# Partition sums of ten modulation vectors: the summed array as stationary operand and two columns as moving one

## Chip, cores and metric

The kernel runs on one core of a Trainium2 chip. The metric is the device time of one execution in microseconds (us). Times of before are the median of 3 runs. One further execution was recorded by the hardware profiler; durations and waits below come from that one.

## What is computed

Two layers of a trunk over 512 latent and 256 context tokens of width 1024, all in float32. The part that matters here is the modulation at the head of each layer:

```python
sc = jax.nn.silu(c)
scc = jax.nn.silu(c_ctx)
for l in range(DEPTH):
    mod_x = (sc @ ada_w[l] + ada_b[l])[:, None, :]
    mod_y = scc @ ada_w[l] + ada_b[l]
    shx1, scx1, gx1, shx2, scx2, gx2 = jnp.split(mod_x, 6, axis=-1)
    shy1, scy1, gy1, shy2, scy2, gy2 = jnp.split(mod_y, 6, axis=-1)
    hx = rms_norm(x, norm1_g[l]) * (1.0 + scx1) + shx1
    hy = rms_norm(y, norm1_g[l]) * (1.0 + scy1) + shy1
...
    x = x + gx1 * (mx @ w_out[l])
```

So each layer multiplies a vector of 1024 (one for latent tokens, one for context tokens) with a 1024x6144 matrix. The result is six vectors of 1024 per kind of token: two shifts (sh1, sh2), two scales (sc1, sc2) and two gates (g1, g2). Shifts and scales are applied where a normalised block stands with features on partitions; gates multiply blocks with tokens on partitions. The rest of a layer is a combined input projection, four kinds of attention or retention ("the mixers" below), an output projection and a SwiGLU feed-forward part with 2816 hidden columns.

## The kernel before

**Projections.** Every large product is float32 made of three float32r products (`mm3`, L465 to L469): high part by high part, high by low, low by high. The low parts are made by `split_unit` (L446) with an ACT copy and a subtraction on DVE or POOL (L213). These products fill TensorE's (PE's) instruction stream from end to end.

**Modulation.** sh1 and sc1 of layer 0 are needed at once and have a path of their own (`ada_first`), which the change leaves alone. The other ten vectors go through `ada_sums` (L371). It works in pieces of 128x512 of the weights: a load on ACT's queue, then on DVE one multiply-add per kind of token (L395 the first, L397 the other seven) into an accumulator of 128x512. After eight pieces one half vector is left as 128 partial sums per column, which have to be added over the partitions. PE does that at L404: for each of four groups of 128 columns, and for each kind of token, the moving operand is the accumulator's 128 columns and the stationary operand is 32 columns of `ones` (a tile of zeros with one column of 1.0, so that token kind s lands in row s). The four groups go to four column tiles of the array (`tile_position=(0, 32*g)`), so that the sums of group g land on PSUM partitions 32g and 32g+1.

Context tokens leave after layer 0, so in layer 1 only sh1 and sc1 have two kinds of token; g1, sh2, sc2 and g2 have one. With two kinds a half vector takes eight products, with one it takes four; each float32 product is two instructions of PE. Below a run of 16 or of 8 such instructions is called a burst: twelve bursts of 16 (g1, sh2, sc2, g2 of layer 0; sh1, sc1 of layer 1; two halves each) and eight of 8.

**After the sums**, `ada_out` (L411) brings a vector into the form in which it is used:
- gates: a tile of zeros (L416, POOL), four loads of the bias (L419, SP's queue), an addition on 128x256 (L421, DVE), four stores to the DRAM tensor `mod_d` (L424, SP's queue). `gate_load` later reads them back, spread over all partitions.
- shifts and scales: a copy out of PSUM (L426, ACT), two transposes of 128x128 (L429, PE), two copies (L431, DVE) and, in `mod_finish`, an addition of the bias for each kind of token (L304, DVE), for scales also a multiply by the norm's gain (L306, DVE).

**Order.** The generators of `ada_sums` are fillers: those of g1 and sh2 run beside the second block of the input projection (columns 1440 to 1951), those of sc2 and g2 beside the block of columns 416 to 927 in the middle of the attention work, and those of layer 1 in the feed-forward part of layer 0 (`steps`, L1442), where the stream of PE is products only. A scheduler then puts the instructions of each engine in a fixed order; an engine works through its own strictly in that order. Tiles get addresses from a planner, and a change of the program moves both.

Of the kernel before, what the change touches and what calls it, by code (L numbers as in the profile page):

```python
# [16 lines left out]
P = 128  # L17
# [70 lines left out]
def build(tc, I, out, opts=None):  # L88
# [81 lines left out]
    AS = (opts or {}).get("as", 1)  # L170
    AD = [(lambda *a, x=x, **k: ada_sums(*a, atag=x, **k)) if x else (lambda *a, **k: ada_rest(*a)) for x in (opts or {}).get("ad", ('ldr', 'ldr'))]
    Q = {k: {"sp": sp, "act": act, "pool": pool}[(opts or {}).get("q", {}).get(k, DQ.get(k, "sp"))]
# [51 lines left out]
    identb = C("identb", [P, P], BF16)  # L224
    ones = C("ones", [P, 33])
    sink = C("sink", [P, LAYERS, H])
# [17 lines left out]
    def vec(name, k0=0, n=1):  # L244
        i, r = VROW[name]
        return vecs[i][:, r + k0:r + k0 + n]
# [52 lines left out]

    def mod_finish(l, v, s, k0, n):  # L300

        m = modT[l][:, s, SLOT[v], k0:k0 + n]
        b = vec("b%d" % l, VT.index(v) * 8 + k0, n)
        dve.tensor_tensor(m, m, b, op=ALU.add)  # L304
        if v[1] == "c":
            dve.scalar_tensor_tensor(m, m, 1.0, vec("g%s_%d" % (v[2], l), k0, n), op0=ALU.add, op1=ALU.mult)  # L306

    def ada_load(q, xs={}):
# [34 lines left out]

    def ada_rest(l, vs, wtag, depth, tag="u"):

        todo = [(v, hf, k) for v in vs for hf in range(2) for k in range(8)]
        W = {}

        def load(i):
            if i < len(todo):  # L350
                v, hf, k = todo[i]
                c0 = VT.index(v) * D + 512 * hf
                W[i] = T(wtag, [P, 512])
                Q["ada"].dma_start(W[i], I["ada_w"][l, k * P:(k + 1) * P, c0:c0 + 512])

        for i in range(depth):
            load(i)
        yield
        for i, (v, hf, k) in enumerate(todo):
            if k == 0 and hf == 0:  # L360
                ps = PS(tag)[:, 0:256]
            w = W.pop(i)
            for g in range(4):
                pe.matmul(ps[32 * g:32 * g + 32, hf * P:hf * P + P], sT[:, k, :], w[:, 128 * g:128 * g + 128],
                          start=(k == 0), stop=(k == 7), tile_position=(0, 32 * g))
            load(i + depth)
            if k == 7 and hf == 1:
                ada_out(l, v, ps, tag)
            yield

    def ada_sums(l, vs, wtag, depth, tag="u", atag="PT", after=None):  # L371
# [16 lines left out]
        for i, (v, hf, k) in enumerate(todo):  # L388
# [10 lines left out]
            if k == 7:  # L399
                if hf == 0:  # L400
                    ps = PS(tag)[:, 0:256]
                for g in range(4):
                    for s in range(ns):
                        pe.matmul(ps[32 * g:32 * g + 32, hf * P:hf * P + P], ones[:, 1 - s:33 - s],  # L404
                                  acc[s][:, 128 * g:128 * g + 128], start=(s == 0), stop=(s == ns - 1),
                                  tile_position=(0, 32 * g))
                if hf == 1:
                    ada_out(l, v, ps, tag)
            yield

    def ada_out(l, v, ps, tag):  # L411
        c0 = VT.index(v) * D
        rt = T(TR[0], [P, 256])
        if v[0] == "g":
            bt = T(TR[1], [P, 2, P])
            pool.memset(bt, 0.0)  # L416
            src = I["ada_b"][l, c0:c0 + D]
            for g in range(4):
                sp.dma_start(bt[32 * g:32 * g + 2],  # L419
                             bass.AP(tensor=src.tensor, offset=src.offset + P * g, ap=[[0, 2], [512, 2], [1, P]]))  # L420
            dve.tensor_tensor(rt, ps, bt.rearrange("p a b -> p (a b)"), op=ALU.add)  # L421
            for g in range(4):
# [388 lines left out]
    for l in range(LAYERS):  # L811
# [620 lines left out]
        v3 = I["ffn_w3"][l].rearrange("(k p) n -> p k n", p=P)  # L1432
        ada_todo = (ada_rest, ada_sums)[AS](1, VT, "qT", 3) if l == 0 else iter(())
        hn = {}
# [103 lines left out]
```

## Time and profile before

| | |
|---|---|
| median of 3 runs | 1904.59 us (1903.46 to 1905.05) |
| profiled execution, its own time | 1910.68 us |
| its span, first to last instruction | 1908.8 us, mean granted PE clock 0.985 |
| PE busy | 1811.7 us, 95% of the span |
| PE weight loads (PEld) | 1494.0 us, 78% |
| DVE busy | 1187.5 us, 62% |
| ACT busy | 672.9 us, 35% |
| POOL busy | 605.2 us, 32% |

PE executes weight loads and products as two streams that overlap. The recorded length of a product holds its way through the array, so that products that follow each other overlap in the record. What one costs in a full stream is therefore read from start to start, not from its length.

### The profile page before, as it was taken

Reading aid. Unit: us, or ns where it says so; the run is one execution under the profiler, and the core shown is the slowest. Engines: PE = TensorE matmul, PEld = TensorE weight load, DVE = VectorE, ACT = ScalarE, POOL = GpSimd, SP = SyncE. Lnnn points to the kernel's source line nnn. Section 1 sums busy time; section 2 is a strip of 40 time slices with the busy share of each in tenths; the row PEclk is TensorE's granted clock in tenths of the full one; section 3 lists DMA queues with packets and bytes.
Section 4 is the critical chain, followed back from the end, with each engine's and each line's share of the span. In section 5 each row is a group of like instructions: output and inputs, shape, how many; then the busy total and the mean of one; then the engine's idle time right before and its main releaser. Section 6 shows DMA issues by size and latency. Waiting matters only on the chain. (4 is left out here: it accounts for less than half of the span.)

```text
span 1908.8 us, 28192 instructions
## 1 busy us (share of the span) xinstructions
PE 1811.7 (95%) x10447; PEld 1494.0 (78%) x10447; DVE 1187.5 (62%) x2676; ACT 672.9 (35%) x1517; POOL 605.2 (32%) x560
## 2 busy tenths in 40 slices
PE   6899999889999999999999999899889999999997
PEld 3677777778889887888888878788777888888885
DVE  5696886877898757564434293465588863434335
ACT  3325643254542221221122233564255532222223
POOL 0211113323115443444344111211333144645542
PEclk9999999899999999999999999999999999999999
DMA  7675436445124346342222222422443033232321
GB/s 226 210 206 162 131 98 187 127 151 117 50 95 127 122 155 199 105 134 63 74 67 67 57 84 91 120 75 81 143 142 100 15 115 101 84 107 89 102 86 44
DMA packets 193555, 215.22 MB, mean 113 GB/s; under 512 B 66660, under 2 KB 141578, under 8 KB 193418
## 3 DMA queue, kind: packets, MB, share of 16 engines
q10 hardware_dynamic: 75840, 111.17, 18.8%
q1 hardware_dynamic: 117578, 102.25, 18.1%
q8 instruction: 82, 1.34, 0.3%
q14 instruction: 55, 0.45, 0.1%
HBM read 192.76 MB, written 20.63 MB: 112 GB/s over the span
## 5 line engine op out<-in xcount | busy, mean ns | idle before, releaser
L469 PE MATMUL pg<-wh,b 128*128 128x512 f32 (+2 forms) x1128 | 439.9, 394 | 7.2 <-POOL b L213 6.2
L467 PE MATMUL pg<-wh,b 128*128 128x512 f32 (+2 forms) x1128 | 443.1, 393 | 1.8 <-ACT b L515 0.9
L468 PE MATMUL pg<-wl,b 128*128 128x512 f32 (+2 forms) x1128 | 441.5, 391 | 2.2 <-DVE rs_yn L288 1.8
L467 PE MATMUL ps<-b,wh 128*128 128x512 f32 (+1 forms) x1120 | 388.2, 347 | 0.0
L469 PE MATMUL ps<-b,wl 128*128 128x512 f32 (+1 forms) x1120 | 386.7, 345 | 0.8 <-DVE wl L213 0.8
L468 PE MATMUL ps<-b,wh 128*128 128x512 f32 (+1 forms) x1120 | 386.9, 345 | 0.5 <-POOL b L213 0.5
L213 DVE TENSOR_TENSOR wl<-raw,wh 128x1024 fp32r<-128x1024 f32 (+1 forms) x131 | 207.4, 1592 | 174.9 <-ACT wh L449 145.3
L449 ACT ACTIVATE wh<-raw 128x1024 fp32r<-128x1024 f32 (+1 forms) x196 | 203.8, 1049 | 271.1 <-PE pg L469 172.3
L213 POOL TENSOR_TENSOR wl<-raw,wh 128x1024 fp32r<-128x1024 f32 (+1 forms) x65 | 160.0, 2462 | 336.7 <-ACT wh L449 286.8
L1362 POOL TENSOR_TENSOR b<-b,nat 128x512 f32<-128x512 f32 (+1 forms) x204 | 217.8, 1087 | 124.0 <-DVE nat L1360 95.0
L469 PEld LDWEIGHTS pg<-wh,b 128*128 128x128 f32 x1128 | 214.9, 191 | 49.6 <-POOL b L213 9.6
L467 PEld LDWEIGHTS pg<-wh,b 128*128 128x128 f32 x1128 | 215.5, 191 | 40.9 <-ACT b L1476 1.9
L468 PEld LDWEIGHTS pg<-wl,b 128*128 128x128 f32 x1128 | 215.2, 191 | 39.7 <-DVE rs_yn L288 2.3
L467 PEld LDWEIGHTS ps<-b,wh 128*128 128x128 f32 x1120 | 213.5, 191 | 27.4 <-issue 2.4
L469 PEld LDWEIGHTS ps<-b,wl 128*128 128x128 f32 x1120 | 213.4, 191 | 26.0 <-DVE wl L213 1.0
L468 PEld LDWEIGHTS ps<-b,wh 128*128 128x128 f32 x1120 | 213.6, 191 | 25.5 <-POOL b L213 0.7
L1360 DVE TENSOR_TENSOR nat<-pg,gate 128x512 f32<-128x512 f32 x240 | 161.9, 688 | 102.0 <-PE pg L469 97.8
L1473 ACT ACTIVATE P<-ps 128x512 f32<-128x512 f32 (+1 forms) x70 | 35.4, 505 | 224.3 <-PE ps L469 128.0
L1475 DVE TENSOR_TENSOR P<-ps,P 128x512 f32<-128x512 f32 (+1 forms) x70 | 40.1, 575 | 118.9 <-PE ps L469 118.8
L1476 ACT ACTIVATE b<-P 128x512 fp32r<-128x512 f32 (+1 forms) x70 | 37.6, 538 | 195.3 <-DVE P L1475 176.0
L397 DVE SCALAR_TENSOR_TENSOR PT<-qT,consts,PT 128x512 f32<-128x512 f32 x112 | 94.0, 857 | 14.6 <-DMA qT<-in_ada_w_dram 13.3
L213 POOL TENSOR_TENSOR b<-P,b 128x512 fp32r<-128x512 f32 (+1 forms) x24 | 27.8, 1158 | 231.9 <-ACT b L1476 231.9
(322 smaller groups left out, 2441.7 us busy)
## 6 DMA issues: line engine op xcount, KB each, us to landing
raw<-in_ffn_w_dram ACTq DMA_DIRECT2D x132, 512.0 KB
qT<-in_ada_w_dram ACTq DMA_DIRECT2D x96, 256.0 KB
raw<-in_w_in_dram SPq DMA_DIRECT2D x40, 512.0 KB
a<-in_ada_w_dram SPq DMA_DIRECT2D x32, 256.0 KB
a<-in_ada_w_dram ACTq DMA_DIRECT2D x32, 256.0 KB
xn<-in_ada_w_dram ACTq DMA_DIRECT2D x32, 256.0 KB
raw<-in_w_out_dram SPq DMA_DIRECT2D x16, 512.0 KB
ldq<-q_d SPq DMA_DIRECT2D x40, 128.0 KB
```

What stands on the lines that cost most here:

```text
L213: eng.tensor_tensor(out, full, hi.bitcast(F32), op=ALU.subtract)
L397: dve.scalar_tensor_tensor(acc[s], w, sS[:, k, s:s + 1], acc[s], op0=ALU.mult, op1=ALU.add)
L449: act.activation(hi, raw_ap, AF.Copy)
L467: pe.matmul(ps, a[0], b[0], start=first, stop=False)
L468: pe.matmul(ps, a[0], b[1], start=False, stop=False)
L469: pe.matmul(ps, a[1], b[0], start=False, stop=last)
L1360: dve.tensor_tensor(tm, ps, gates[(0 if t < 4 else 2) + b], op=ALU.mult)
L1362: eng.tensor_tensor(ap, ap, tm[:, a:c], op=ALU.add)
L1473: act.activation(s1[j][:, sl], ps, AF.Silu)
L1475: dve.tensor_tensor(s1[j][:, sl], ps, s1[j][:, sl], op=ALU.mult)
L1476: act.activation(gh[j][:, sl], s1[j][:, sl], AF.Copy)
```

## The change

In `ada_sums` the two operands change places. The accumulator's 128x128 group becomes the stationary operand, and two columns of `ones` (now 4 wide) become the moving one; no `tile_position` is given. The sums of a group then land on 128 PSUM partitions, in two columns (one per kind of token), which is the form in which shifts and scales are used. The number of products stays the same.

`ada_out` follows. A bias is read from `vecs`, where all biases already stand as columns. Shifts and scales need one addition straight from PSUM, and scales one multiply; copy, transposes and `mod_finish` are gone. Gates add the bias into a tile of 128x16, transpose it once (PE), copy the 16x128 result (ACT), and store it in two transfers; the tile of zeros and the four loads are gone. `ada_rest`, which no option in use selects, is deleted.

```diff
@@ ada_sums
                 if hf == 0:
-                    ps = PS(tag)[:, 0:256]
+                    ps = PS(tag)[:, 0:16].rearrange("p (k s) -> p k s", s=2)
                 for g in range(4):
                     for s in range(ns):
-                        pe.matmul(ps[32 * g:32 * g + 32, hf * P:hf * P + P], ones[:, 1 - s:33 - s],
-                                  acc[s][:, 128 * g:128 * g + 128], start=(s == 0), stop=(s == ns - 1),
-                                  tile_position=(0, 32 * g))
+                        pe.matmul(ps[:, 4 * hf + g, :], acc[s][:, 128 * g:128 * g + 128], ones[:, 1 - s:3 - s],
+                                  start=(s == 0), stop=(s == ns - 1))
@@ ada_out
-        rt = T(TR[0], [P, 256])
+        b = vec("b%d" % l, VT.index(v) * 8, 8).unsqueeze(1).to_broadcast([P, 2, 8])
+        sums = ps.rearrange("p k s -> p s k")
         if v[0] == "g":
-            bt = T(TR[1], [P, 2, P])
-            pool.memset(bt, 0.0)
-            src = I["ada_b"][l, c0:c0 + D]
-            for g in range(4):
-                sp.dma_start(bt[32 * g:32 * g + 2],
-                             bass.AP(tensor=src.tensor, offset=src.offset + P * g, ap=[[0, 2], [512, 2], [1, P]]))
-            dve.tensor_tensor(rt, ps, bt.rearrange("p a b -> p (a b)"), op=ALU.add)
-            for g in range(4):
-                dst = mod_d[l][:, c0:c0 + D].rearrange("s (h g f) -> s h g f", h=2, g=4)[:, :, g, :]
-                sp.dma_start(dst, rt[32 * g:32 * g + 2, :].rearrange("p (a b) -> p a b", a=2))
+            m = S("adag", 16, bufs=2)
+            dve.tensor_tensor(m.rearrange("p (s k) -> p s k", s=2), sums, b, op=ALU.add)
+            pt = PS(tag)[0:16, 0:P]
+            pe.transpose(pt, m, ident)
+            rt = T(TR[0], [P, P])[0:16, :]
+            act.activation(rt, pt, AF.Copy)
+            for s in range(2):
+                sp.dma_start(mod_d[l][s, c0:c0 + D].rearrange("(k f) -> k f", f=P), rt[8 * s:8 * s + 8, :])
         else:
-            act.activation(rt, ps, AF.Copy)
-            pt = PS(tag)[:, 0:256].rearrange("p (a b) -> p a b", a=2)
-            for b in range(2):
-                pe.transpose(pt[:, b, :], rt[:, b * P:(b + 1) * P], ident)
-            for s in range(2):
-                dve.tensor_copy(modT[l][:, s, SLOT[v]].rearrange("p (h g) -> p h g", h=2), pt[:, :, s::32])
-                mod_finish(l, v, s, 0, 8)
+            m = modT[l][:, :, SLOT[v]]
+            dve.tensor_tensor(m, sums, b, op=ALU.add)
+            if v[1] == "c":
+                dve.scalar_tensor_tensor(m, m, 1.0, vec("g%s_%d" % (v[2], l), 0, 8).unsqueeze(1).to_broadcast([P, 2, 8]),
+                                         op0=ALU.add, op1=ALU.mult)
```

The scheduler's order moves with it. In the first place below, PE's order in the feed-forward part of layer 0 behind the second half of sc1 of layer 1 (`PT` are accumulators, `consts` holds `ones` and the identity, `ps` are the products of the feed-forward part), before:

```order
L404 MATMUL pu_7576<-PT_7585,consts 32x128
L404 MATMUL pu_7576<-PT_7586,consts 32x128
L467 MATMUL ps_7977<-b_1446_6238,wh_7873 128x512
L468 MATMUL ps_7977<-b_1448_6240,wh_7873 128x512
L469 MATMUL ps_7977<-b_1446_6238,wl_7874 128x512
L429 MATMUL pu_7961<-consts,nat_7959 128x128 x2
L467 MATMUL ps_7977<-b_1446_6238,wh_7873 128x512
```

and after, where lines from `ada_out` on have smaller numbers (L467 to L469 have become L429 to L431, and the sums stand at L369):

```order
L369 MATMUL pu_7543<-consts,PT_7552 128x2
L369 MATMUL pu_7543<-consts,PT_7553 128x2
L429 MATMUL ps_7935<-b_1444_6213,wh_7840 128x512
L430 MATMUL ps_7935<-b_1446_6215,wh_7840 128x512
L431 MATMUL ps_7935<-b_1444_6213,wl_7841 128x512
L429 MATMUL ps_7935<-b_1444_6213,wh_7840 128x512
```

The sums stand at the same place in PE's order, and the two transposes behind them are gone.

The second place is PE's order behind the second half of g1 of layer 1, in the same part, before:

```order
L469 MATMUL ps_8429<-b_1447_6239,wl_8327 128x512
L404 MATMUL pu_8103<-PT_8164,consts 32x128 x4
L467 MATMUL ps_8481<-b_1418_6094,wh_8332 128x256
L468 MATMUL ps_8481<-b_1419_6095,wh_8332 128x256
L469 MATMUL ps_8481<-b_1418_6094,wl_8333 128x256
```

and after:

```order
L431 MATMUL ps_8387<-b_1445_6214,wl_8285 128x512
L369 MATMUL pu_8061<-consts,PT_8122 128x2 x4
L429 MATMUL ps_8435<-b_1416_6069,wh_8290 128x256
L430 MATMUL ps_8435<-b_1417_6070,wh_8290 128x256
L431 MATMUL ps_8435<-b_1416_6069,wl_8291 128x256
L384 MATMUL pu_8425<-consts,adag_8423 16x128
```

Here a transpose has come in, three products behind the sums; it reads a tile that DVE writes in between.

The third place is DVE's order at the end of the first gate, g1 of layer 0 (`ldq` are accumulators, `a` pieces of weights, `pu` the sums), before:

```order
L395 TENSOR_SCALAR ldq_1174<-a_237_1131,consts 128x512
L421 TENSOR_TENSOR nat_1053<-pu_971,nat_1054 128x256
L395 TENSOR_SCALAR ldq_1175<-a_237_1131,consts 128x512
```

and after:

```order
L362 SCALAR_TENSOR_TENSOR ldq_991<-a_210_1015,consts,ldq_991 128x512
L1155 TENSOR_SCALAR kd_2994<-kd_2994 128x8
L382 TENSOR_TENSOR adag_1053<-pu_971,consts 128x16
L360 TENSOR_SCALAR ldq_1095<-a_211_1022,consts 128x512
```

The addition has moved up by one half vector: it now stands almost directly behind the multiply-add that completes the accumulator (`ldq_991`) from which PE makes its sums, where before it stood behind all of the next vector's first half. In the mixers of layer 0 the order of all engines shifts in many small places; from the feed-forward part of layer 0 on, PE's order differs only where sums and transposes stand.

## Rows read from the trace of the kernel before

**Rows 1.** Busy us by stretch: PE, PEld, DVE, ACT, POOL; PEclk, DMA share, GB/s.

```profile
96.00:143.00 47.00, 45.51 (x245) 33.48 (x244) 43.37 (x72) 13.51 (x37) 6.18 (x2) 1.00 0.73 206
220.00:312.00 92.00, 88.64 (x636) 67.79 (x635) 76.70 (x201) 45.92 (x144) 10.04 (x8) 1.00 0.39 119
312.00:430.00 118.00, 104.61 (x601) 88.42 (x600) 85.83 (x307) 47.90 (x127) 40.12 (x49) 0.91 0.50 154
617.00:993.00 376.00, 368.88 (x2018) 312.73 (x2017) 214.59 (x276) 74.30 (x105) 167.10 (x156) 1.00 0.37 116
```

**Rows 2.** Groups of the sums' line L404, layer 1 (columns: count, ns min/median/max, first and last start).

```profile
L404 PE MATMUL pu<-PT,consts x128: 272/273/298, 615.8 to 992.4; 128*32 128x128 f32 x128
```

**Rows 3.** Timeline of PE, a burst of 16 (start us, us, operation, partitions and columns).

```profile
615.48 0.28 PE L468 MATMUL ps<-b,wh 128*128 128x256 f32 x1
615.60 0.28 PE L469 MATMUL ps<-b,wl 128*128 128x256 f32 x1
615.80 0.66 PE L404 MATMUL pu<-PT,consts 128*32 128x128 f32 x16
...
616.73 0.39 PE L468 MATMUL ps<-b,wh 128*128 128x512 f32 x1
616.96 0.39 PE L469 MATMUL ps<-b,wl 128*128 128x512 f32 x1
```

**Rows 4.** The same view, a burst of 8.

```profile
740.71 0.28 PE L469 MATMUL ps<-b,wl 128*128 128x256 f32 x1
...
741.62 0.40 PE L468 MATMUL ps<-b,wh 128*128 128x512 f32 x1
```

**Rows 5.** The same view, a burst of layer 0, which stands in two pieces.

```profile
97.78 0.39 PE L467 MATMUL pg<-wh,b 128*128 128x512 f32 x1
98.10 0.41 PE L404 MATMUL pu<-ldq,consts 128*32 128x128 f32 x2
...
99.10 0.66 PE L404 MATMUL pu<-ldq,consts 128*32 128x128 f32 x14
...
100.02 0.60 PE L693 MATMUL pu<-consts,nat 128*128 128x128 f32 x4
```

**Rows 6.** Timeline of PE's weight loads in the retention part: float32, 128 columns.

```profile
366.52 0.53 PEld L1282 LDWEIGHTS ps<-ldr,P 128*128 128x128 f32 x4
366.97 0.30 PEld L1278 LDWEIGHTS ps<-b,rt 128*128 128x128 f32 x2
367.19 0.19 PEld L1282 LDWEIGHTS ps<-ldr,P 128*128 128x128 f32 x1
```

**Rows 7.** Timeline of PE, the way out of such a run into products.

```profile
355.75 0.43 PE L467 MATMUL pg<-wh,b 128*128 128x416 f32 x1
356.02 0.35 PE L468 MATMUL pg<-wl,b 128*128 128x416 f32 x1
356.20 0.35 PE L469 MATMUL pg<-wh,b 128*128 128x416 f32 x1
```

**Rows 8.** Timeline of PE, a pair of the transposes that go.

```profile
141.07 0.40 PE L468 MATMUL pg<-wl,b 128*128 128x512 f32 x1
...
141.76 0.39 PE L467 MATMUL pg<-wh,b 128*128 128x512 f32 x1
```

**Rows 9.** Waits in 617 to 993 us (total, times, longest us).

```profile
PE pu L429 <- ACT nat L426: 3.5, 2, 2.7
```

**Rows 10.** Timeline of ACT ahead of the longer of these waits.

```profile
723.35 0.38 ACT L1473 ACTIVATE P<-ps 128x256 f32<-128x256 f32 x1 [7.32 <-DVE PT L395]
```

**Rows 11.** Busy time by stretch, columns as in the first group: a stretch at half clock.

```profile
569.85:573.25 3.40, 3.40 (x18) 3.40 (x18) 2.14 (x6) 0.42 (x1) 0.73 (x1) 0.50 0.06 24
337.75:354.80 17.05, 12.43 (x54) 11.10 (x54) 11.99 (x37) 1.47 (x3) 1.40 (x3) 0.50 0.26 77
```

**Rows 12.** Groups of lines L421 and L424 (columns as in the second group).

```profile
L421 DVE TENSOR_TENSOR nat<-pu,nat x4: 420/424/425, 121.8 to 992.8; 128x256 f32<-128x256 f32 x4
L424 SPq DMA_DIRECT2D mod_d<-nat x16: 232/255/283, 122.3 to 994.2; - x16
```

More of the change, by code (lines that the diff above doesn't have):

```diff
@@ L170, in build @@
     AS = (opts or {}).get("as", 1)
-    AD = [(lambda *a, x=x, **k: ada_sums(*a, atag=x, **k)) if x else (lambda *a, **k: ada_rest(*a)) for x in (opts or {}).get("ad", ('ldr', 'ldr'))]
+    AD = [lambda *a, x=x, **k: ada_sums(*a, atag=x, **k) for x in (opts or {}).get("ad", ('ldr', 'ldr'))]
     Q = {k: {"sp": sp, "act": act, "pool": pool}[(opts or {}).get("q", {}).get(k, DQ.get(k, "sp"))]
@@ L224, in build @@
     identb = C("identb", [P, P], BF16)
-    ones = C("ones", [P, 33])
+    ones = C("ones", [P, 4])
     sink = C("sink", [P, LAYERS, H])
@@ L298, in build @@
     SLOT = {"sh1": 0, "sc1": 1, "sh2": 2, "sc2": 3}
[L300 to L306, printed above, removed]
     def ada_load(q, xs={}):
@@ L342, in ada_first @@
                                  op0=ALU.add, op1=ALU.mult)
[L344 to L360, printed above, removed]
-                ps = PS(tag)[:, 0:256]
-            w = W.pop(i)
-            for g in range(4):
[L364 to L369, printed above, removed]
     def ada_sums(l, vs, wtag, depth, tag="u", atag="PT", after=None):
@@ L412, in ada_out @@
         c0 = VT.index(v) * D
-        rt = T(TR[0], [P, 256])
+        b = vec("b%d" % l, VT.index(v) * 8, 8).unsqueeze(1).to_broadcast([P, 2, 8])
+        sums = ps.rearrange("p k s -> p s k")
         if v[0] == "g":
-            bt = T(TR[1], [P, 2, P])
-            pool.memset(bt, 0.0)
-            src = I["ada_b"][l, c0:c0 + D]
-            for g in range(4):
-                sp.dma_start(bt[32 * g:32 * g + 2],
-                             bass.AP(tensor=src.tensor, offset=src.offset + P * g, ap=[[0, 2], [512, 2], [1, P]]))
-            dve.tensor_tensor(rt, ps, bt.rearrange("p a b -> p (a b)"), op=ALU.add)
-            for g in range(4):
-                dst = mod_d[l][:, c0:c0 + D].rearrange("s (h g f) -> s h g f", h=2, g=4)[:, :, g, :]
-                sp.dma_start(dst, rt[32 * g:32 * g + 2, :].rearrange("p (a b) -> p a b", a=2))
-        else:
-            act.activation(rt, ps, AF.Copy)
-            pt = PS(tag)[:, 0:256].rearrange("p (a b) -> p a b", a=2)
-            for b in range(2):
-                pe.transpose(pt[:, b, :], rt[:, b * P:(b + 1) * P], ident)
-            for s in range(2):
-                dve.tensor_copy(modT[l][:, s, SLOT[v]].rearrange("p (h g) -> p h g", h=2), pt[:, :, s::32])
-                mod_finish(l, v, s, 0, 8)
+            m = S("adag", 16, bufs=2)
[6 more added lines that the diff above has]
+                sp.dma_start(mod_d[l][s, c0:c0 + D].rearrange("(k f) -> k f", f=P), rt[8 * s:8 * s + 8, :])
+        else:
+            m = modT[l][:, :, SLOT[v]]
[3 more added lines that the diff above has]
+                                         op0=ALU.add, op1=ALU.mult)
     def gate_load(l, v):
@@ L1432, in build @@
         v3 = I["ffn_w3"][l].rearrange("(k p) n -> p k n", p=P)
-        ada_todo = (ada_rest, ada_sums)[AS](1, VT, "qT", 3) if l == 0 else iter(())
+        ada_todo = ada_sums(1, VT, "qT", 3) if l == 0 else iter(())
         hn = {}
```

1 line of the change is left out of this document (removed).

## The prediction

> **What bounds the kernel now.** I read the busy time by stretch first, then the starts of PE's instructions around the sums, then waits and other engines. In the stretches where the sums run, PE is busy 45.5 of 47 us and 88.6 of 92 us in the mixers of layer 0, and 368.9 of 376 us in the feed-forward part [rows 1]. No other engine comes near, except DVE in the first of them (43.4 of 47). So what the sums take from PE there is paid almost in full, and work taken from DVE, ACT, POOL or the DMA queues is worth nothing by itself unless PE waits for it.
>
> The length of a product in the record says nothing here: one of the sums is shown with 273 ns [rows 2], yet sixteen of them pass in well under a microsecond, because four column tiles work side by side. What counts is the time from the product ahead of a burst to the second one behind it, less what those products need among their own kind. That covers two losses too: the start of a burst is late, and so is the second product behind it.
>
> - Burst of 16: from 615.60 to 616.73 are 1.13 us. A product of 256 columns needs 0.12 of it (615.48 to 615.60), one of 512 columns 0.23 (616.73 to 616.96). The burst costs 0.78 us [rows 3].
> - Burst of 8: 0.91 - 0.35 = 0.56 us [rows 4].
> - Burst of layer 0, in two pieces (2 and 14) with products between: from 97.78 to 100.02 are 2.24 us with four products of 512 columns in them, so 2.24 - 0.92 = 1.32 us [rows 3, 5].
>
> The feed-forward part has four whole bursts of 16 and eight of 8 (64 float32 products, the 128 instructions of [rows 2]). Layer 0 has eight bursts of 16, which I cost all like the one shown. Before, then: 4 x 0.78 + 8 x 0.56 = 7.6 us and 8 x 1.32 = 10.6 us, together 18.2 us.
>
> **The sums after the change.** Their number stays 256 instructions. What each streams falls from 128 columns to two, but what it loads rises from 32 columns to 128, and the four tiles that worked side by side are gone, so that every load has the whole array. The kernel has such loads of float32 data already, in the retention part. Four loads take from 366.52 to 366.97, two more to 367.19: 0.67 us for six, 0.112 us each [rows 6]. By the code the products at L1278 stream 128 columns and those at L1282 stream 64, and the loads keep one pace through both. So it is the load that sets the pace, and streaming less buys nothing. On the way out, the first product behind such a run is followed after 0.27 us, where 0.18 is usual: 0.09 us are lost [rows 7].
>
> - Burst of 16: 16 x 0.112 + 0.09 = 1.88 us. Burst of 8: 0.99 us. Burst in two pieces (PE's order still has one product ahead and seven behind): 1.79 + 2 x 0.09 = 1.97 us.
> - Feed-forward part: 4 x 1.88 + 8 x 0.99 = 15.4, less 7.6: **+7.8 us**.
> - Mixers of layer 0: 8 x 1.97 = 15.8, less 10.6: **+5.2 us**.
>
> The ends for this price: the cheapest that rows show is a load-and-product pair of today's bursts (0.78 / 16 = 0.05 us), by which the sums would cost what they cost now, +0; the dearest is a load that waits for its predecessor's whole way, which no row shows; I bound it by adding the 0.11 us of a further load to each, 256 x 0.11 = 28 us more. I take 0.112, since those loads are of the same type and width and alternate with products already; for that reason I give the dear end hardly any chance.
>
> **What goes from PE.** Six pairs of transposes (L429). One pair costs 141.76 - 141.07 - 2 x 0.23 = 0.23 us [rows 3, 8], six 1.4 us. Twice PE also stood in front of them until ACT had copied the sums out, 3.5 us in all, the longer time 2.7 [rows 9]. ACT was late because it had itself stood 7.3 us until DVE's L395, the first multiply-add into a new accumulator, was done [rows 10]; the change leaves that standstill on ACT, but nothing on PE waits for it any more, as the copy L426 is gone for shifts and scales. What is late next is ACT's copy for gates, and only a store to DRAM waits for that. **-4.9 us** together.
>
> **What comes to PE.** Four transposes of one instruction: 0.23 less one pace of 0.11 is 0.12 us each, +0.5 us. Each reads what DVE adds behind the sums, three products later in PE's order. DVE's addition began 0.4 us behind the last sum (992.4 to 992.8) and took 0.42 us for 256 columns; 16 columns need no longer [rows 2, 12]. So the transpose can go at the latest 0.8 us behind the burst. In the feed-forward part three products of 0.12 and the way out cover 0.45 of that, leaving a wait between 0 and 0.4 us; I take 0.2, twice: +0.4 us. In layer 0 the three products are of 0.23, and cover it. **+0.9 us** together.
>
> **What changes elsewhere.** The other engines get less work: DVE four additions of 0.42 us replaced by small ones and most of the small copies gone, ACT six copies, POOL four clears, SP 24 of 32 transfers at about 0.26 us [rows 12]. I cost all of it at nothing, because PE is the bound in these stretches. If that cover were gone, SP's 24 transfers would be worth 6 us at most. Between the ends 0 and -6 I take 0. The store of a gate now goes behind a longer chain (sums, addition, transpose, copy), so SP, which works in order, stands there up to 2 us longer with loads behind it; but its queue holds six transfers fewer per gate. I cost this at 0 as well.
>
> **Sum.** 7.8 + 5.2 - 4.9 + 0.9 = **+9.0 us**. The profiled execution took 1910.68 us, 6.1 above the median of 1904.59; by it the changed kernel would take 1919.7, and in terms of the median **1913.6 us**. A measurement of this kernel can tell about 0.2% (3.8 us) from no change, so this is slower.
>
> **Rivals.**
>
> *Cheap loads (faster side).* If a load of 128 columns hides in part when almost nothing streams, the pace falls. The change breaks even where the sums cost 18.2 + 4.0 = 22.2 us; less 28 ways out at 0.09, that leaves 0.077 us per instruction. At the cheapest pace above the sums cost what they do now, and the kernel gains 4.0 us: 1900.6. For it speaks that no row has loads with so short a stream; against it that the pace did not move between 64 and 128 columns. Chance 0.07.
>
> [...]
>
> *The mixers give it back.* The scheduler's order shifts all over the mixers of layer 0. PE's idle time in the two filler stretches is 1.5 + 3.4 = 4.9 us [rows 1]; if the longer bursts fall into it, +5.2 becomes +0.3 and the time 1908.7. Behind them, from 312 to 430 us, PE idles 13.4 us and stands at half clock for 17 us with 12.4 us of work in it [rows 1, 11]; an order that spares this gains up to 6.2 us more: 1902.5. Nothing in the change aims there, so it can as well go the other way. Chance 0.23: 0.16 within 0.2%, 0.07 below.
>
> *The clock falls, or DVE becomes the bound.* During a burst almost nothing streams. A stretch at half clock lasts 3.4 us and costs half, 1.7 us [rows 11]. If four bursts in the mixers set one off, +6.8: 1920.4; all twelve long ones, 1934. Against it: through the load-bound run of rows 6 the loads kept the pace of the full clock, and the feed-forward part, dense on both sides of each burst, stood at 1.00 throughout [rows 1]. [...]
> In the same stretch DVE, 3.6 us short of full [rows 1], now adds directly behind the sums and stands until PE has made them, about 2.3 us per vector (1.88 and the 0.4 above), with the next vector's multiply-adds queued behind; two vectors are 4.6, one more than DVE has to spare. That adds 1 us or, with the later fillers, up to 4. Chance of clock or waits together 0.13, at 1918 to 1930.
>
> **How the numbers follow.** The forecast itself, 1909.5 to 1918, has 0.57. Slower by over 0.2%: 0.57 + 0.13 = 0.70. Within 0.2%: 0.16. Faster: 0.07 + 0.07 = 0.14. The range 1904 to 1922 leaves out the cheap loads (0.07), most of the lucky orders (0.05) and the worst clock (0.05).
>
> **What would show it.** Right: in the feed-forward part, weight loads of L369 follow each other every 0.11 us, a burst of 16 takes near 1.9 us and one of 8 near 1.0; the wait of PE for ACT's copy is gone; granted clock there 1.00; PE's time from 617 us to the end of the feed-forward part grows by about 4 us. Wrong: loads closer than 0.08 us, half-clock stretches behind bursts, or a mixer stage of layer 0 that ends earlier than before by more than the bursts add.

## The result and the profile after

The changed kernel took 1927.59 us (median of 4, 1926.55 to 1930.86); the kernel before, run beside it, 1904.82 (median of 4). The ratio is 1.0119, 95% interval 1.0101 to 1.0138: about 22.8 us slower, where 9.0 were forecast and the range ended at 1922. The direction was right; the size was not, and the range did not hold the time.

The profiled execution took 1926.55 us, 1 us below the median, where that of before lay 6 above its own. So the two traces differ by 15.9 us only. The busy times of the page:

```profile
PE 1826.2 (95%) x10439; PEld 1517.4 (79%) x10439; DVE 1187.1 (62%) x2655; ACT 671.6 (35%) x1515; POOL 601.6 (31%) x556
```

**The bursts.** Timeline of PE around the first burst of 16 in the feed-forward part, one of 8, and the first of layer 0 (start us, us, operation, partitions and columns):

```profile
630.21 0.28 PE L431 MATMUL ps<-b,wl 128*128 128x256 f32 x1
630.33 1.84 PE L369 MATMUL pu<-consts,PT 128*128 128x2 f32 x16
632.04 0.47 PE L429 MATMUL ps<-b,wh 128*128 128x512 f32 x1
632.35 0.39 PE L430 MATMUL ps<-b,wh 128*128 128x512 f32 x1
...
755.67 0.28 PE L431 MATMUL ps<-b,wl 128*128 128x256 f32 x1
755.79 0.95 PE L369 MATMUL pu<-consts,PT 128*128 128x2 f32 x8
756.60 0.47 PE L429 MATMUL ps<-b,wh 128*128 128x512 f32 x1
756.91 0.39 PE L430 MATMUL ps<-b,wh 128*128 128x512 f32 x1
...
95.93 0.39 PE L429 MATMUL pg<-wh,b 128*128 128x512 f32 x1
96.16 0.28 PE L369 MATMUL pu<-consts,ldq 128*128 128x2 f32 x2
...
97.07 1.62 PE L369 MATMUL pu<-consts,ldq 128*128 128x2 f32 x14
98.56 0.48 PE L430 MATMUL pg<-wl,b 128*128 128x512 f32 x1
98.88 0.39 PE L431 MATMUL pg<-wh,b 128*128 128x512 f32 x1
```

Counted as the prediction counted [rows 3 to 5]: the burst of 16 costs 632.35 - 630.21 - 0.35 = 1.79 us, that of 8 costs 1.24 - 0.35 = 0.89, that of layer 0, with five products of 512 columns in it, 2.95 - 1.15 = 1.80. Inside, an instruction follows the other after (632.04 - 630.33) / 16 = 0.107 us, where the retention's loads had given 0.112.

**The feed-forward part**, from the first sum of its first burst to the first sum of its last (busy us by stretch, columns as in [rows 1]), after and before:

```profile
630.40:1007.70 377.30, 373.96 (x2021) 323.32 (x2020) 211.10 (x261) 73.10 (x102) 164.53 (x154) 1.00 0.37 116
```
```profile
615.80:992.30 376.50, 369.38 (x2029) 313.14 (x2028) 214.86 (x275) 74.30 (x105) 167.60 (x157) 1.00 0.37 116
```

The last burst of 8 is left out of both. The stage grew by 0.8 us: PE works 4.6 us more and idles 3.8 us less (3.3 after, 7.1 before). The granted clock was 1.00 in both. Of PE's waits there only these are left (total, times, longest us); that of [rows 9] is gone:

```profile
PE pg L431 <- DVE b L213: 1.6, 1, 1.6
PE pg L431 <- POOL b L213: 1.1, 2, 0.5
PE pg L429 <- ACT b L1438: 0.6, 2, 0.3
```

So of the 15.9 us between the traces the stage that holds twelve of the twenty half vectors made 0.8. What follows it grew by 0.5. The other 14.6 arose before 630 us, in the mixers of layer 0. I split these at one product that both traces have (at 280.0 us before, 285.4 after). The same view, before first, with one of its half-clock stretches (the others are in [rows 11]):

```profile
60.00:280.00 220.00, 208.16 (x1354) 160.30 (x1350) 181.65 (x442) 106.49 (x300) 30.14 (x28) 0.98 0.54 157
280.00:615.80 335.80, 315.62 (x2016) 266.72 (x2015) 268.37 (x732) 143.07 (x363) 100.39 (x105) 0.96 0.40 121
416.20:419.60 3.40, 3.40 (x10) 2.72 (x9) 3.40 (x15) 2.64 (x6) 0.74 (x1) 0.51 0.88 305
```

and after, with all its half-clock stretches from 285 to 630 us:

```profile
60.00:285.40 225.40, 210.13 (x1351) 167.71 (x1349) 181.32 (x434) 107.09 (x301) 29.63 (x26) 0.98 0.52 153
285.40:630.40 345.00, 324.44 (x2016) 273.40 (x2016) 269.78 (x732) 141.77 (x362) 102.37 (x105) 0.95 0.39 117
288.90:292.30 3.40, 3.40 (x10) 2.68 (x10) 0.79 (x3) 0.99 (x2) 0.00 (x0) 0.52 0.39 123
343.50:364.00 20.50, 16.72 (x61) 14.53 (x62) 15.28 (x46) 2.66 (x6) 3.98 (x4) 0.50 0.38 125
387.90:391.30 3.40, 3.40 (x11) 3.08 (x11) 1.25 (x7) 1.21 (x3) 2.10 (x3) 0.52 0.15 49
428.80:435.60 6.80, 6.21 (x16) 4.84 (x16) 6.34 (x25) 4.12 (x13) 1.28 (x1) 0.51 0.90 296
568.80:572.20 3.40, 3.40 (x19) 3.40 (x18) 3.40 (x8) 2.71 (x6) 1.28 (x1) 0.52 0.37 129
```

The first stretch is 5.4 us longer: 3.4 of it idle time (15.3 against 11.8), while half-clock stretches take 6.8 us of it in both (3.4 us lost before, 3.0 after). The second is 9.2 us longer, and by the last burst of g2 at 315 us the kernel is through with all sums of layer 0. PE idles alike there (20.6 against 20.2 us). But it works 33.1 us at half clock (the sum of the five rows) where before it worked 19.2 (12.43 and 3.40 of [rows 11], and 3.40 above). Half of that is lost: 16.6 against 9.6, so 7.0 of the 9.2 us are clock. One wait of the first stretch that has grown (before, the longest at this line was 1.0 us), and how the clock goes behind it (timeline of PE; the products' pace goes from 0.23 to 0.43):

```profile
152.99 0.69 PE L548 MATMUL pt<-consts,P 128*128 128x128 f32 x2 [3.50 <-DVE P L582]
...
153.91 0.63 PE L431 MATMUL pg<-wh,b 128*128 128x512 f32 x1
154.34 0.63 PE L429 MATMUL pg<-wh,b 128*128 128x512 f32 x1
```

DVE's waits from 60 to 322 us have two rows that before had not, or hardly:

```profile
DVE adag L382 <- PE pu L369: 5.4, 2, 3.0
...
DVE ldr L360 <- PE pu L369: 2.8, 1, 2.8
```

DVE stands at the gates' additions until PE has made the sums, as the prediction's third rival said. Three causes were therefore open for the surplus in the mixers: the **form** (longer bursts, DVE standing, the store behind a longer chain), the **order** into which the scheduler shifted, and the **clock**, either set off by the bursts or following from the order.

### The profile page after: what moved, and what is told of

Its sections match the earlier page's. It is cut to its first block, busy times and chain, and to the rows that moved or that the text cites. A ratio compares the mean times of both kernels' runs of the same rounds, so it can differ in the third digit from the quotient of the medians.

```text
span 1924.7 us, 28131 instructions
## 1 busy us (share of the span) xinstructions
PE 1826.2 (95%) x10439; PEld 1517.4 (79%) x10439; DVE 1187.1 (62%) x2655; ACT 671.6 (35%) x1515; POOL 601.6 (31%) x556
## 5 line engine op out<-in xcount | busy, mean ns | idle before, releaser
L429 PE MATMUL pg<-wh,b 128*128 128x512 f32 (+2 forms) x1128 | 442.9, 393 | 5.2 <-DVE nat L1178 2.5
L431 PE MATMUL pg<-wh,b 128*128 128x512 f32 (+2 forms) x1128 | 440.3, 394 | 7.0 <-POOL b L213 5.4
L429 PE MATMUL ps<-b,wh 128*128 128x512 f32 (+1 forms) x1120 | 387.1, 346 | 0.0
L431 PE MATMUL ps<-b,wl 128*128 128x512 f32 (+1 forms) x1120 | 386.2, 345 | 0.8 <-DVE wl L213 0.8
L431 PEld LDWEIGHTS pg<-wh,b 128*128 128x128 f32 x1128 | 215.5, 191 | 48.0 <-POOL b L213 8.3
L429 PEld LDWEIGHTS pg<-wh,b 128*128 128x128 f32 x1128 | 215.6, 191 | 43.8 <-DVE nat L1178 2.7
L431 PEld LDWEIGHTS ps<-b,wl 128*128 128x128 f32 x1120 | 213.2, 190 | 26.1 <-DVE wl L213 1.0
L429 PEld LDWEIGHTS ps<-b,wh 128*128 128x128 f32 x1120 | 213.2, 190 | 25.1
L362 DVE SCALAR_TENSOR_TENSOR PT<-qT,consts,PT 128x512 f32<-128x512 f32 x112 | 89.5, 821 | 11.5 <-DMA qT<-in_ada_w_dram 10.2
```

The costliest lines, as they stand in the source:

```text
L362: dve.scalar_tensor_tensor(acc[s], w, sS[:, k, s:s + 1], acc[s], op0=ALU.mult, op1=ALU.add)
L429: pe.matmul(ps, a[0], b[0], start=first, stop=False)
L431: pe.matmul(ps, a[1], b[0], start=False, stop=last)
```

## The experiments

Ratios are to the kernel before, run beside each kernel on the same chip. Its medians there were 1906.5 to 1907.9 us, where beside the changed kernel it took 1904.8; so two kernels of different rounds are compared by their ratios as well as by their times. Executions of one and the same kernel lie up to 13 us apart (e11: 1902.0 to 1914.8), and each run has one trace; how far two traces of one order agree is said below.

| run | what | median us | ratio, 95% interval |
|---|---|---|---|
| e1 | only layer 1 new | 1911.2 | 1.0017 (1.0004 to 1.0030) |
| e2 | only layer 0 new | 1927.0 | 1.0095 (1.0078 to 1.0111) |
| e6 | only the gates of layer 0 new | 1917.3 | 1.0049 (1.0033 to 1.0066) |
| e3 | before, one more copy | 1909.9 | 1.0011 (0.9999 to 1.0024) |
| e8 | before, one more copy, late | 1908.4 | 1.0006 (0.9994 to 1.0018) |
| e11 | before, DVE stands for the sums | 1907.8 | 0.9996 (0.9979 to 1.0012) |
| e14 | before, late order of the changed kernel in part | 1911.2 | 1.0025 (1.0012 to 1.0038) |
| e4 | changed, one more copy | 1926.2 | 1.0087 (1.0069 to 1.0104) |
| e5 | changed, bias of gates on POOL | 1929.9 | 1.0119 (1.0100 to 1.0137) |
| e7 | changed, other late order in part | 1927.6 | 1.0111 (1.0094 to 1.0128) |
| e9 | changed, without the context tokens' sums in layer 0 | 1919.2 | 1.0053 (1.0029 to 1.0077) |
| e10 | changed, way out 4 pieces later | 1925.2 | 1.0086 (1.0066 to 1.0105) |
| e12 | changed, sums of layer 0 twice | 1945.4 | 1.0185 (1.0157 to 1.0213) |
| e13 | changed, late order of before | 1914.1 | 1.0039 (1.0027 to 1.0051) |
| e15 | changed, a third late order | 1914.8 | 1.0047 (1.0034 to 1.0060) |

### Which vectors: e1, e2, e6

```diff
+    def NEW(l, v):
+        return l == 1                      # e1
+        return l == 0                      # e2
+        return l == 0 and v[0] == "g"      # e6
...
+                        if NEW(l, v):
+                            pe.matmul(ps[:, 4 * hf + g, :], acc[s][:, 128 * g:128 * g + 128], ones[:, 1 - s:3 - s],
+                                      start=(s == 0), stop=(s == ns - 1))
+                            continue
...
+        (ada_out_new if NEW(l, v) else ada_out_old)(l, v, ps, tag)
```

> Layer 0 keeps the old sums and the old way out, layer 1 (its ten half vectors of sums stand in the feed-forward part of layer 0, between products) takes the new ones. The trace of the changed kernel says that the feed-forward part became 0.8 us longer and what follows it 0.5 us: all theories expect 1906 (1904.8 + 1.3), up to 1910 if the waits that PE no longer has were worth less than they seem. If instead the whole surplus were a price of the new sums themselves, twelve of the twenty half vectors (four bursts of 16 and eight of 8) would carry about half of it: 1916.

> The other half: layer 0 new, layer 1 old. If the loss sits in the mixers of layer 0, as the trace says: 1904.8 + 21 = 1926. If new sums cost the same wherever they stand: 1914.

> The kernel before with the new form only for the two gates of layer 0 (g1, g2), everything else old. If the gates' way out (DVE behind the sums, the store behind a longer chain) is the cause: nearly all of the loss, 1922 to 1927. If each burst costs alike: half of it, about 1916 to 1917. If it is the shifts' and scales' form: below 1911.

Layer 1 alone adds 3.2 us, layer 0 alone 18.1, together 21.3 of the 22.8 measured for the change: the loss sits in the mixers. Two of the four vectors there make 9.3, half of it, which none of the expectations for e6 but "each alike" gives. But eight longer bursts at +0.48 us (1.80 less 1.32) are 3.8 us, not 18.

### A nudge of the order: e3, e4, e8, e7

The scheduler works with times of its own, so that a copy that nobody reads can move its order. Some 0.07 us was reckoned for one (in the trace of before, two copies of 128x8 at L431 took 0.23 us, where one is recorded with 0.16).

```diff
+    nz = C("nz", [P, 2])
...
             na_table_load()
+            dve.tensor_copy(nz, Vyn[:, 1, 0:2])     # e3 on before, e4 on the changed kernel
...
+            if l == 0:
+                dve.tensor_copy(nz, nt[:, 0:2])     # e8: on before, ahead of the retention's states
...
+                if l == 0:
+                    dve.tensor_copy(nz, ov[:, 0:2]) # e7: on the changed kernel, in ret_chunk
```

> The kernel before with one more copy of 128x2 on DVE at the start of the filler stretch (some 0.07 us, its result is not used). The scheduler's order moves with it in 165 places of PE's list in the mixers of layer 0. If the order alone is worth many microseconds (theory of the order), the time moves by 4 us or more, rather upward, to 1909 to 1925. If what counts is the work and the waits that the change brings (theory of the sums), it stays within 2 us: 1903 to 1907.

> The changed kernel with the same extra copy; its order moves in 44 places of PE's list in the mixers. Theory of the order: moves by 4 us or more, either way, from 1927.6. Theory of the sums: within 2 us, 1926 to 1930.

> The changed kernel with an extra copy of 128x2 on DVE in each chunk of retention of layer 0 (some 0.07 us each, result not used): the order moves behind the last sums only (15 places of PE's list). Theory of the order: the 7 to 8 us that the changed kernel loses between 315 and 630 us, where no sum stands any more, move by 2 us or more. Otherwise, within 1 us there; total 1926 to 1929.

> The kernel before with one extra copy of 128x2 on DVE ahead of the retention's states of layer 0: the order moves in the retention and behind it only (22 places of PE's list, 81 rows). Theory of the order: that stretch gets longer by 2 us or more, 1910 to 1915. Otherwise within 1 us, 1907 to 1909.

None moved the median by 4 us (by the ratios e4 lies 6 us below the changed kernel, with intervals that touch), and I took that for a blow to the theory of the order. It was none: from some 930 rows of PE's list on, e4 has the order of the changed kernel, and e7 changes it at some 15 places only. All kernels with new gates up to here shared one late order of PE, e2, e4 and e5 exactly, e7 nearly, e6 from some 440 us on, and all lost 4 to 8 us between 315 and 630 us (from products that they share with before); no kernel with the old form had done so up to here. Form and order could not be told apart this way.

### DVE behind the sums: e5, e10, e11

```diff
+            raw = S("adar", 16, bufs=2).rearrange("p (s k) -> p s k", s=2)      # e5
+            act.activation(raw, sums, AF.Copy)
-            dve.tensor_tensor(m.rearrange("p (s k) -> p s k", s=2), sums, b, op=ALU.add)
+            pool.tensor_tensor(m.rearrange("p (s k) -> p s k", s=2), raw, b, op=ALU.add)
...
+        late = []                                                               # e10
...
-                    ada_out(l, v, ps, tag)
+                    late.append((i + 4, l, v, ps, tag))
+            if late and (l == 1 or i >= late[0][0] or i + 1 == len(todo)):
+                ada_out(*late.pop(0)[1:])
...
+        if l == 0:                                                              # e11, on before
+            dve.tensor_copy(nz, ps[:, 0:2])
```

> The changed kernel, but for gates ACT copies the sums out of PSUM (128x16) and POOL adds the bias, so DVE, which stood 5.4 us at the additions of the two gates of layer 0 (3.0 the longest) with the next vector's multiply-adds queued behind, no longer stands there. The order of the engines is otherwise nearly that of the changed kernel (25 rows of PE's list differ). If DVE's standing at the gates is the cause (theory of the new wait): the mixers get 4 to 6 us back, 1921 to 1923. If it lies in the order behind the sums and in the clock: within 2 us of 1927, with the same half-clock stretches behind 315 us.

> The changed kernel, with the way out of each vector of layer 0 written four weight pieces later, so that DVE's addition stands behind multiply-adds of the next vector and finds the sums ready. Theory of the way out: DVE no longer stands 5.4 us at the gates and 1.4 at sh2, and 6 to 9 us come back, 1918 to 1921. Theory of the length: no change, 1925 to 1929.

> The kernel before with one small copy on DVE out of the sums (128x2) at the head of the way out of each vector of layer 0, result not used: DVE now stands for the sums in the old form too, four times. Theory of the way out: 5 us or more are lost, 1912 to 1916. Theory of the length: 1906 to 1909, since the bursts are the old ones.

e5 took DVE's wait away and got a new one in its place: the transpose of the gate stood in PE's order and waited for POOL (PE's waits, 60 to 322 us).

```profile
PE pu L386 <- POOL adag L384: 5.5, 1, 5.5
```

Its time stayed where it was. e10 missed its aim: DVE stood 7.6 us at the gates instead of 5.4, so its -2.4 us (some -6 by the ratios) say nothing on the question. e11 says more. There DVE stood longer for the old sums than in the changed kernel at all its additions (5.4 us at the gates and 1.4 at sh2), and the time did not move (DVE's waits, same stretch):

```profile
DVE consts L414 <- PE pu L405: 8.3, 3, 5.3
```

The order of PE moved with that copy too (at some 120 places behind 220 us), so this is no clean zero. But e13 below stands longer at the gates as well, and is 13 us faster than the changed kernel. So DVE standing for sums is not what makes the surplus.

### The length of the bursts: e9, e12

```diff
-                    for s in range(ns):
+                    for s in range(1 if l == 0 else ns):            # e9
...
-                                  start=(s == 0), stop=(s == ns - 1))
+                                  start=(s == 0), stop=(l == 0 or s == ns - 1))
...
-                for g in range(4):
+                for g in (0, 1, 2, 3) * (2 if l == 0 else 1):       # e12
```

> The changed kernel without the sums for context tokens in layer 0 (their columns come out as zero), so that a burst there has 8 instructions instead of 16 and lasts 0.8 us instead of 1.6: less than before (1.3). All else stays, the way out and the additions of DVE directly behind the sums too. Theory of the length (a burst in the mixers costs what it lasts on PE, and more by what it sets off): 7 us less by itself, 1920; if longer bursts are also what brings the waits and the half-clock stretches, 1908 to 1912. Theory of the way out (DVE standing behind the sums): 1924 to 1927. Theory of the order and the clock: the half-clock time stays near 76 to 82 us, where the kernel before has 58 to 62, and the time near 1922.

> The changed kernel with every sum of layer 0 made twice into the same place, so that a burst there has 32 instructions, 1.7 us more, eight times 1.7 = 13.6 us. Theory of the length, paid once: 1941. If longer bursts set off waits and half-clock stretches in proportion to their length: 1950 or more. Theory of the way out: DVE stands 1.7 us longer per vector as well, 1941 to 1946. Theory of the order: anything between 1927 and 1945, as part of the longer bursts falls into idle time.

With 8, 16 and 32 instructions per burst the medians are 1919.2, 1927.6 and 1945.4. From end to end that is 26.2 us for 8 x 24 instructions, 0.136 us each, where the pace is 0.107. So length is paid a little more than once (the order moved in e9 and in e12 as well). Part of the rest is the clock, and e12 shows how. Timeline of PE at its fourth burst, and busy times (columns as in [rows 1]) of 3.5 us of the second burst and of the half-clock stretch behind it:

```profile
149.42 3.40 PE L369 MATMUL pu<-consts,ldq 128*128 128x2 f32 x30
152.68 0.48 PE L430 MATMUL pg<-wl,b 128*128 128x512 f32 x1
...
153.46 0.63 PE L429 MATMUL pg<-wh,b 128*128 128x512 f32 x1
153.89 0.63 PE L430 MATMUL pg<-wl,b 128*128 128x512 f32 x1
```
```profile
115.50:119.00 3.50, 3.50 (x33) 3.46 (x32) 0.15 (x2) 0.00 (x0) 0.00 (x0) 1.00 0.33 90
119.70:123.10 3.40, 3.40 (x11) 2.70 (x10) 3.40 (x7) 0.27 (x1) 0.00 (x0) 0.56 0.42 128
```

PE has no idle time in either, and still the clock falls: at seven of the eight bursts of 32 a half-clock stretch begins in the burst or at most 1.3 us behind it. At bursts of 16 it is rarer, and in the feed-forward part of the changed kernel it never happens (clock 1.00 from 630.40 to 1007.70 us). In layer 0 of the changed kernel it is one of eight (288.90 above, behind a burst ahead of which PE had also waited 1.2 us). Over the eight kernels that have the new form in all of layer 0 and bursts of 16 there (the changed one, e2, e4, e5, e7, e10, e13, e15) it is 11 of 64; over the six with the old bursts there (before, e1, e3, e8, e11, e14) it is 1 of 48. In ten of the eleven PE had been idle for 0.8 to 2.1 us of the 5 us ahead of the fall; in e13 at 126.8 us only for 0.15. So the rival of the falling clock is real for this change too: at 1.7 us each, some 2 us per kernel (an estimate from these counts). It is not the surplus, since e13, with two such falls, is the faster one. And e9, with bursts shorter than those before, is still 10.1 us slower than before, 3.2 of them for layer 1. So length is not the surplus either.

### Form and order crossed: e13, e14, e15

Three edits of no weight of their own were meant to give the two missing corners, and a third order.

```diff
+        late = []                                              # e13, on the changed kernel
...
-                    ada_out(l, v, ps, tag)
+                    late.append((i + 1, l, v, ps, tag))
+            if late and (l == 1 or i >= late[0][0] or i + 1 == len(todo)):
+                ada_out(*late.pop(0)[1:])
...
+        if l == 0:                                             # e14, on before (e11 has one copy)
+            for _ in range(2):
+                dve.tensor_copy(nz[:, 0:2], ps[:, 0:2])
...
-            rt = T(TR[0], [P, P])[0:16, :]                     # e15, on the changed kernel
+            rt = T("P", [P, P])[0:16, :]
```

> The changed kernel with the way out of each vector of layer 0 written one weight piece later. With it the scheduler falls back, from some 260 us on, to the very order of PE that the kernel before has in the rest of the mixers of layer 0 (no row differs between there and the feed-forward part but sums and transposes). Theory of the order: the 9 us that the changed kernel loses between 260 and 630 us shrink to 1 or 2 (the second burst of sc2 and those of g2 stand there), and the whole to 1918 to 1921. Theory of the form (the gates' way out, the store behind a longer chain, the stationary sums): nothing changes there, 1925 to 1929.

> The other corner: the kernel before, with two small copies of 128x2 on DVE at the head of the way out of each vector of layer 0 (results not used; the run with one such copy took 1907.8). With two, the scheduler falls into PE's order of the changed kernel from some 280 us to the feed-forward part. Theory of the order: 5 to 7 us are lost there with the old sums too, 1912 to 1915, and the half-clock time rises. Theory of the form: 1906 to 1909.

> The changed kernel with one edit of no weight of its own: the 16x128 result of a gate's transpose lies in a tile of another tag (P). The late order is a third one, which the run of the kernel before with one copy per way out (1907.8) shares in its last part. Theory of the order: the stretch from 315 to 630 us gets back 4 to 8 us, 1920 to 1924. Theory of the form: 1925 to 1929.

e13 has the whole change and takes 1914.1 us, 13.5 less than the changed kernel (15 by the ratios), although DVE stands longer for the gates (7.2 us in its waits, against 5.4).

Read row by row from the traces, with sums and transposes of the modulation left out, the corners are not quite what was expected of them. e13 has PE's order of before from 336 us on, not from 260. e14 has that of the changed kernel only from 435 us on (25 products stand elsewhere in the 26 us ahead of that); earlier it has an order of its own, no nearer to the changed kernel's than to that of before.

So I cut the late part at two products ahead of which all four kernels have done the same work, and end it at the last product ahead of the feed-forward part's first burst. Busy times of the two stretches, before first, then changed:

```profile
287.25:410.33 123.08, 111.86 (x669) 92.50 (x668) 87.22 (x280) 43.48 (x112) 37.68 (x48) 0.93 0.45 141
410.33:615.60 205.27, 197.81 (x1313) 169.58 (x1311) 174.86 (x437) 95.52 (x237) 62.17 (x57) 0.98 0.37 109
294.12:421.76 127.64, 116.69 (x669) 96.62 (x668) 86.76 (x292) 44.18 (x123) 38.78 (x47) 0.91 0.42 132
421.76:630.21 208.45, 199.92 (x1310) 170.01 (x1310) 177.62 (x433) 94.78 (x231) 63.40 (x58) 0.98 0.36 106
```

e13, with its half-clock stretches there:

```profile
291.04:413.95 122.91, 112.04 (x670) 93.72 (x669) 85.58 (x290) 44.83 (x123) 35.55 (x47) 0.93 0.43 133
413.95:617.17 203.22, 195.86 (x1312) 168.07 (x1311) 175.03 (x437) 95.75 (x237) 62.07 (x57) 0.99 0.38 110
341.80:358.90 17.10, 12.21 (x53) 10.87 (x53) 12.10 (x32) 1.47 (x3) 3.04 (x3) 0.50 0.24 77
420.30:423.70 3.40, 3.40 (x10) 2.61 (x9) 3.40 (x12) 3.12 (x8) 1.22 (x1) 0.50 0.88 287
```

and e14, the old form:

```profile
285.71:409.12 123.41, 111.87 (x668) 92.01 (x667) 86.81 (x285) 44.16 (x119) 38.96 (x47) 0.94 0.45 142
409.12:618.24 209.12, 199.29 (x1310) 170.17 (x1309) 178.25 (x434) 94.38 (x231) 63.49 (x60) 0.98 0.35 104
338.00:351.70 13.70, 12.08 (x51) 10.86 (x48) 10.62 (x39) 1.56 (x4) 0.85 (x2) 0.52 0.31 93
416.50:423.30 6.80, 6.28 (x17) 4.96 (x17) 6.70 (x27) 4.88 (x15) 1.28 (x1) 0.53 0.83 245
573.50:576.90 3.40, 3.40 (x19) 3.40 (x19) 3.40 (x10) 0.42 (x1) 0.78 (x1) 0.55 0.42 148
```

The stretch between the two products (287.25 to 410.33 us of before), in us:

| form | order of PE | length | PE idle | lost at half clock |
|---|---|---|---|---|
| old (before) | old | 123.1 | 11.2 | 6.2 |
| new (e13) | old from 336 us on | 122.9 | 10.9 | 6.1 |
| old (e14) | its own | 123.4 | 11.5 | 6.0 |
| new (changed) | new | 127.6 | 11.0 | 10.1 |

and from the second product (410.33 us of before) to the feed-forward part:

| form | order of PE | length | PE idle | lost at half clock |
|---|---|---|---|---|
| old (before) | old | 205.3 | 7.5 | 3.4 |
| new (e13) | old | 203.2 | 7.4 | 1.7 |
| old (e14) | new but for 25 products | 209.1 | 9.8 | 4.8 |
| new (changed) | new | 208.5 | 8.5 | 4.8 |

(Idle is length less PE's busy time; lost is half of PE's busy time in the half-clock rows.) e1 and e2, whose orders here are row for row those of before and of the changed kernel, repeat the lengths to 1.8 us in the first stretch (121.7 and 125.9) and to 0.1 in the second (205.2 and 208.5).

In the second stretch the crossing is clean: the new order costs 3.9 us with the old form and 5.2 with the new one, and the new form costs nothing in either. In the first stretch the changed kernel alone is slower, by 4.6 us, 3.8 of them lost clock. There the new form in the old order loses nothing; the old form in the changed kernel's order was not run.

e15, with a third order, is 12.8 us below the changed kernel (13.7 by the ratios). So the same form, in three orders, measures 1.0119, 1.0047 and 1.0039: the surplus over the forecast comes with the order, not with the form. Much of it is clock: PE idles for about as long in all four kernels, but not in the same pieces, and behind some the clock stays down longer. The order alone does not settle the clock, though. e5 has the order of the changed kernel from 230 to 630 us, on PE row for row and on DVE, ACT and POOL but for one place, and takes 333.4 us for the two stretches against 336.1, with 8.2 us lost at half clock against 14.9 (it had lost 5.5 us to its new wait, at 119 us):

```profile
296.65:630.03 333.38, 310.94 (x1978) 261.04 (x1977) 264.30 (x722) 139.57 (x357) 102.31 (x106) 0.97 0.39 117
348.50:365.60 17.10, 13.25 (x53) 11.20 (x52) 12.20 (x37) 1.56 (x4) 2.42 (x3) 0.50 0.39 132
430.40:433.80 3.40, 3.10 (x9) 2.40 (x10) 3.35 (x12) 2.53 (x7) 1.29 (x1) 0.50 0.93 296
```

As a whole e14 costs the old form 4.8 us in the medians, where the order is worth 13 to 15 with the new form. Since its order is not that of the changed kernel everywhere, it stays open whether the old form would lose as much in the very same order, or whether the longer bursts fit that order worse. The addresses of tiles can move with each of these edits too, and were not held.

## Why the prediction was right in direction and wrong in size

- **Price of the bursts: right.** 0.107 us per instruction against 0.112; 1.79, 0.89 and 1.80 us against 1.88, 0.99 and 1.97. The way out loses 0.08 us (632.35 - 632.04 - 0.23), where 0.09 was taken; the rest of the difference is the pace. Feed-forward part 4 x 1.01 + 8 x 0.33 = +6.7 (7.8 said), layer 0 8 x 0.48 = +3.8 (5.2 said). A load of 128 columns goes with each instruction now; those of before, with loads of 32 columns and four column tiles, cost 0.78 / 16 = 0.05 us each.
- **Transposes and waits: right.** The wait of [rows 9] is gone, and PE idles 3.8 us less in the feed-forward part. The new transposes found their tile ready: the 0.4 us for them did not come up (PE's waits above have no row for L384).
- **Feed-forward part: +0.8 us against +4.0.** The mechanism held. 1.1 of the difference is the bursts, 0.4 the wait that did not come, and 0.3 the last burst of 8, which stands outside of the stretch; the rest, some 1.4 us, I have not placed.
- **The form as a whole.** With the measured bursts the sum is 6.7 + 3.8 - 4.9 + 0.5 = +6.1. e13, whose late order is that of before, measures +7.4 (5.1 to 9.7). The forecast of 9.0 lies in that interval; it reckoned with nothing for the order. That its sum fits is in part luck: the feed-forward part gave 3 us less than forecast, e13's order ahead of 336 us is not that of before, and falls of the clock behind bursts (some 2 us) had no term in it.
- **The step that failed** is the order of the mixers, which the sum put at nothing. "I cost all of it at nothing, because PE is the bound in these stretches" holds only as far as PE never waits there, and of the shift of order the second rival priced the gain alone: "it can as well go the other way" had no price and no part of the range. In its place the runs showed 13 to 15 us: the changed kernel against e13 and e15, which have the same form in another order. The profile held it: in the mixers PE idled 32 us and lost 13.0 at half clock (9.6 and 3.4 above), and what moves there is waits and clock, not work. The changed kernel has +3.8 us of idle time and +6.6 of lost clock from 60 us to the feed-forward part, 10.4 of the 14.6; the other 4.2 are work, where 5.0 were forecast (5.2 and two transposes, less two pairs).
- **The third rival, half right.** DVE did stand behind the sums as described, and no cost of it could be made out (e11, e13). Bursts do bring the clock down, those of 32 at seven of eight places (e12), those of 16 in layer 0 at 11 of 64 places, which is worth some 2 us a kernel and not the 6.8 of four bursts.
- **The range** was too narrow above: its upper end took the clock by four bursts and stopped there. The kernels with the new form in both layers (the changed one, e4, e5, e7, e10, e13, e15) lie between 1.0039 and 1.0119, those with the old form throughout (e3, e8, e11, e14) between 0.9996 and 1.0025. With the new form the orders tried differ by up to 0.8%, with the old one by 0.3%.

## What to carry to other kernels

Where a scheduler sets the order, an edit has two prices: its own, which the rows of the trace gave here to within 2 or 3 us, and that of the new order, which they do not give. Here the second arose where the busiest engine still idles and its clock moves; in the feed-forward part, where PE is busy nearly without a gap (373.96 of 377.30 us), the order hardly moved and nothing of the kind was seen. Copies of no weight on the old kernel did not show its size ahead: they spread over 0.3%, while the change itself moved by 0.8% between orders. And before an edit is judged slower by its form, it should be run under more than one order: the same change was worth +0.4% or +1.2%.

## What was not expected of the hardware

TensorE's granted clock fell from 1.00 to about half (0.50 to 0.56 in the half-clock rows above, the pace of a 512-column product going from 0.23 to 0.43 us) behind bursts in which PE is recorded as busy without a gap: 32 instructions with two moving columns and loads of 128 columns, most of them in a piece 3.3 us long, did it at seven of eight places (e12), and 16 such instructions at 11 of 64, mostly with a wait of PE close ahead. The busy time of the record did not tell of the fall ahead of it: in e12 PE was busy for all of the 3.50 us from 115.50 us on, and over the 3.40 us from 119.70 us on the clock was 0.56. What the clock follows, no run here shows.
